# Hybrid decoder trunk step: recalibrated planner, FP32 stages in any unit, convolution as a side job

## The chip, the cores and the metric

The kernel runs on one core of one Trainium2 chip. The metric is the device time of one execution in microseconds (us), the median of several runs; less is better. Everything is computed in float32.

## The reference, cut to what matters

One layer on 256 prompt rows and 8 x 8 sample rows (T = 320 rows of 2048 columns). The parts that the change touches:

```python
def mixer_projections(x, g_mix, w_in, g_q_swa, g_k_swa, g_q_x):
    z = rmsnorm(x, g_mix) @ w_in
    b, c, hc, q, k, v, qx = jnp.split(z, IN_SPLITS, axis=-1)
    ...
    return b, c * hc, q, k, v, qx

def short_conv(u_ext, w):                  # CONV_K = 3 taps, 512 columns
    out = w[0] * u_ext[:, 0:length]
    for i in range(1, CONV_K):
        out = out + w[i] * u_ext[:, i:i + length]
    return out

y_conv = b * short_conv(u_ext, conv_w)     # u_ext: u = c * hc behind two earlier rows
y_swa = swa_prompt(...) / swa_sample(...)  # window 128, rel_bias(dist, table), sinks
y_x = cross_attention(qx, mk, mv)          # 256 memory tokens, 4 heads
x = x + concat([y_conv, y_swa, y_x]) @ w_out
x = x + jnp.square(relu(rmsnorm(x, g_mlp) @ w_up)) @ w_down
```

The new convolution rows and the keys and values of the windows are returned as well.

## The kernel before, in words

Activations lie transposed, 128 features on the partitions and the 320 rows along the free side. Each large product is made of three F32R matmuls (high x high, high x low, low x high). The weights come in pieces of 256 x 512 (512 KB). ACT copies a piece to its high part (`wh`), DVE subtracts that to give its low part (`wl`, `split_piece`, lines 415 to 447). There are four raw buffers and four split buffers; the load of a piece into a raw buffer is issued on SP's queue behind the DVE operation that frees the buffer.

The weights' columns are worked through in groups of 512: x-queries, keys and values, memory keys, memory values, queries (two groups), then C, H, B of the convolution, then w_out, w_up, w_down. A group is a list of units. A standard unit is 12 matmuls of 320 columns; a unit of the memory groups is 6 matmuls of 512 columns. `run_unit` (486) writes a unit's matmuls into the program, then splits a further piece, and then `boundary` (478) writes what has been held back: evacuations of PSUM, low parts, and one `step` of the side jobs.

All smaller work is side jobs: Python generators (heads' norms, the bias table, the memory's norm, attention of prompt and samples, outputs) that `Side.step` (218) advances once behind each unit. A `yield n` sleeps n steps. A job's small matmuls thus stand in TensorE's queue between two units, and each engine works through its queue in the order in which the program was written.

When a job may go on is decided while the program is written, by a planner's clock, the class `Pace` (93). It keeps one clock for each engine and one for the transfers; `cost` (106) gives the time of an operation, `load` (135) that of a transfer: bytes at a rate, and then `LAG` more until the tile counts as landed (2.0 for raw weights). `after(*tiles)` (272) lets a job sleep until all its tiles are written by 0.2 us or more on TensorE's planned clock. `bank(every)` (276) fetches a PSUM bank for a small product; with `every=2`, the default, only at an even step. The loops at 885 and 919 (memory attention of the samples) also wait for an even step.

Jobs that the prediction speaks of: `x_job` (563) splits x and ends at step 7. `bias_job` (1062) starts at step 8: a DVE memset of the tile `z`, POOL's loads of the table into it and of a one-hot matrix into `w`, `yield 4`, `after`, a bank, then one product of 33 rows. `cross_sample` (863) has four batches of keys and four of values, two 256 KB tiles each; the first two batches are loaded at the start, each later one when a batch has been used. `h_evac` (1153) takes a column block of h out of PSUM, multiplies it with C's block and forms the three taps of the convolution; behind its fourth block it starts `conv_out_job` (1170), which issues an output on POOL's queue. `pre_late` (1220) issues the copies of the old caches (out_old_k, out_old_v) on the same queue. `b_evac` (1182) needs the convolution's result. `zs` are ten tiles for such results.

Of the kernel before, what the change touches and what calls it, by code (L numbers as in the profile page):

```python
# [12 lines left out]
ALU = mybir.AluOpType  # L13
AX = mybir.AxisListType

P = 128
# [15 lines left out]
NEG = -1e30  # L32

NW2 = 12
LAG = 6.0
WARM = 10
C_B, C_C, C_H, C_Q, C_K, C_V, C_X = 0, 512, 1024, 1536, 2560, 2816, 3072

# [54 lines left out]
class Pace:  # L93
# [12 lines left out]
    def cost(self, eng, op, out, ins):  # L106
        n = max(a.free_size() for a in [out] + ins)
        if eng == "pe":
            n = out.free_size()
            if ins[0].dtype == F32R:  # L110
                return 0.0033 + n / 2400.0
            quarter = 0.25 if out.partition_size() == 32 else 1.0
            return 0.0009 * n if op == "transpose" else max(0.11, n / 600.0) * quarter
        if eng == "act":
            return 0.1 + n * 0.00083
        if eng == "dve":
            return 0.08 + n * 0.00104
        return 0.1 + n * 0.0025

    def issue(self, eng, op, out, ins):  # L120
# [13 lines left out]

    def load(self, out):
        start = max(self.clock["dma"], self.clock["pe"])
        self.clock["dma"] = start + out.free_size() * 4 * out.partition_size() / 330e3
        self.wrote[out.name] = (self.clock["dma"] + (2.0 if out.name.startswith("raw") else LAG), "dma")

    def ready(self, tiles):  # L140
# [6 lines left out]
class Paced:  # L147
# [3 lines left out]
    def __getattr__(self, op):  # L151
        f = getattr(self.engine, op)
        if not callable(f) or op == "preload_act_table_set":
            return f

        def issue(*args, **kw):
            aps = [a for a in list(kw.values()) + list(args) if isinstance(a, bass.AP)]
            out = kw["out"] if "out" in kw else args[0]
            if op == "dma_start":
                if out.name not in self.pace.dram:  # L160
                    self.pace.load(out)
            else:
                if "accum_out" in kw:
                    self.pace.wrote[kw["accum_out"].name] = (self.pace.clock[self.name] + 0.5, self.name)
                self.pace.issue(self.name, op, out, [a for a in aps if a is not out])
            return f(*args, **kw)  # L166

        return issue
# [79 lines left out]
def trunk_step(ctx: ExitStack, tc: tile.TileContext, I, O):  # L248
    nc = tc.nc
    pace = Pace()  # L250
    side = Side(NW2, pace)
# [16 lines left out]
    ax = Slots(axp, "ax", 4, pace.idle)  # L268
    zs = Slots(zp, "z", 10)
# [3 lines left out]
        while not pace.ready(tiles):  # L273
            yield 1

    def bank(every=2):

        while side.now % every:
            yield 1
        t = ax.get([P, 512])  # L280
        while t is None:
            yield every
            t = ax.get([P, 512])
        return t

    def zt(cols=336):
        return zs.need([P, 336])
# [43 lines left out]
    def gcol(name, i=0):  # L331
        return cols[:, col[name] + i:col[name] + i + 1]
# [6 lines left out]
    st = {}  # L339
# [233 lines left out]
    def mean_rsqrt(out, sq):  # L573

        yield from after(sq)
        bk = yield from bank(1)
        yield from mean_over(bk, sq, mean_d)
        y = yield from zt()
        yield from newton_terms(y[:, 0:T], out, bk[:, 0:T])
        ax.put(bk)  # L580
        dve.tensor_scalar(out=y[:, 0:T], in0=y[:, 0:T], scalar1=-0.5, scalar2=None, op0=ALU.mult)
        dve.scalar_tensor_tensor(out=out, in0=out, scalar=-3.0, in1=y[:, 0:T], op0=ALU.add, op1=ALU.mult)
        zs.put(y)
# [52 lines left out]
    def start_head(name, ps, gain, dest):  # L636
        early = "rb" not in side.flags
        home = w2 if early else zs
        z = home.must([P, 336])
        if early:  # L640
            side.held += 1
            act.activation(out=z[:, 0:T], in_=ps, func=AF.Copy)
        else:
            dve.tensor_tensor(out=z[:, 0:T], in0=ps, in1=rb, op=ALU.mult)

        def gen():
            if early:
                while "rb" not in side.flags:
                    yield 1
                dve.tensor_tensor(out=z[:, 0:T], in0=z[:, 0:T], in1=rb, op=ALU.mult)  # L650
            while side.now < turn[0] or turn[1] == 2:
                yield 1
            turn[0] = side.now + 2
            turn[1] += 1
            y = yield from zt()
            yield from after(z)
            act.activation(out=y[:, 0:T], in_=z[:, 0:T], func=AF.Square)
            yield 1
            yield from after(y)
            bk = yield from bank(1)  # L660
            yield from mean_over(bk, y[:, 0:T], mean_h)
            a = yield from zt()
            yield from newton_terms(y[:, 0:T], a[:, 0:T], bk[:, 0:T])
            ax.put(bk)
            dve.scalar_tensor_tensor(out=z[:, 0:T], in0=z[:, 0:T], scalar=gain, in1=y[:, 0:T],
                                     op0=ALU.mult, op1=ALU.mult)
            zs.put(y)
            dest(lambda out, v: dve.scalar_tensor_tensor(out=out, in0=v(a), scalar=-3.0, in1=v(z),
                                                         op0=ALU.add, op1=ALU.mult))
            zs.put(a)  # L670
            home.put(z)
            side.held -= int(early)
            turn[1] -= 1

        side.add(name, gen())
# [131 lines left out]
    def cross_prompt(h):  # L807
        yield from after(st["qxT"])
        split_both(lambda m: m[:, 4 + h, 0:TP], st["qxT"][:, h, :])
        yield 1  # L810
        yield from after(S1l[:, 4 + h, :], S1l[:, 0, :])
        bk = yield from bank(1)
        for t in range(2):
            three(bk[:, t * 256:(t + 1) * 256], [m[:, 4 + h, t * P:(t + 1) * P] for m in (S1h, S1l)],
                  [m[:, h, 0:MEM] for m in (S1h, S1l)], True, True)
        yield 1
        p = yield from half()
        den = sm()
        cut = [slice(t * 256, (t + 1) * 256) for t in range(2)]
        yield from cross_softmax([(p[:, c], bk[:, c]) for c in cut], den)  # L820
        ax.put(bk)
        yield from after(p)
        bk = yield from bank()
        for kb in range(2):
            for t in range(2):
                pe.transpose(bk[:, kb * 256 + t * P:kb * 256 + (t + 1) * P],
                             p[:, t * 256 + kb * P:t * 256 + (kb + 1) * P], ident)
        yield 1
        w2.put(p)
        pt = []  # L830
        for _ in range(2):
            t = yield from w2.need([P, 512], F32R)
            pt.append(t)
        act.activation(out=pt[0], in_=bk, func=AF.Copy)
        dve.tensor_tensor(out=pt[1], in0=bk, in1=pt[0].bitcast(F32), op=ALU.subtract)
        ax.put(bk)
        yield from after(pt[1])
        bk = yield from bank(1)
        for kb in range(2):
            v = [m[:, 8 + kb * 2 + h // 2, h % 2 * P:(h % 2 + 1) * P] for m in (S1h, S1l)]  # L840
            three(bk[:, 0:TP], v, [t[:, kb * 256:(kb + 1) * 256] for t in pt], kb == 0, kb == 1)
        yield 1
        w2.put(*pt)
        yield from put_mix(lambda m: m[:, 12 + h, 0:TP], bk[:, 0:TP])
        ax.put(bk)
# [17 lines left out]
    def cross_sample(f):  # L863
# [18 lines left out]
        for b in range(4):  # L882
            cur = queue.pop(0)
            yield from after(*cur)
            while side.now % 2:
                yield 1
            for h in range(XH):
                pe.matmul(out=sb[h * 32:(h + 1) * 32, 0:MEM], lhsT=qm[:, h * P + b * 32:h * P + b * 32 + 32],
                          rhs=cur[h // 2][:, (h % 2) * MEM:(h % 2 + 1) * MEM], start=b == 0, stop=b == 3,
                          tile_position=(0, h * 32), skip_group_check=True)  # L890
            w2.put(*cur)
            yield from load()
# [23 lines left out]
        for b in range(4):  # L916
            cur = queue.pop(0)
            yield from after(*cur)
            while side.now % 2:
                yield 1  # L920
            for kb in range(2):
                for h in range(XH):
                    c = h * 32
# [229 lines left out]
    def h_evac(m, ps):  # L1153
# [5 lines left out]
        dve.tensor_tensor(out=u[:, m, 2:258], in0=z[:, 0:TP], in1=u[:, m, 2:258], op=ALU.mult)  # L1159
        us = usample(m)[:, :, 2:10]  # L1160
        dve.tensor_tensor(out=us, in0=per_batch(z[:, TP:T]), in1=us, op=ALU.mult)
        dve.tensor_scalar(out=z, in0=u[:, m, 0:336], scalar1=gcol("conv_w", m), scalar2=None, op0=ALU.mult)
        for i in (1, 2):
            dve.scalar_tensor_tensor(out=z, in0=u[:, m, i:i + 336], scalar=gcol("conv_w", 4 * i + m), in1=z,
                                     op0=ALU.mult, op1=ALU.add)
        st["y"][m] = z
        if m == 3:
            side.add("convout", conv_out_job())

    def conv_out_job():  # L1170
        cu = yield from zt()
# [8 lines left out]
        yield 1  # L1180

    def b_evac(m, ps):
        side.until(["cp"])
        y = st["y"][m]
        z = zs.must([P, 336])
        dve.tensor_tensor(out=z[:, 0:T], in0=ps, in1=rb, op=ALU.mult)
# [217 lines left out]
```

## Time and profile before

| | |
|---|---|
| median of 3 runs | 1320.77 us (1320.54 to 1321.83) |
| the profiled execution, its own time | 1322.82 us |
| its span | 1320.7 us |
| TensorE (PE) busy | 1311.3 us, 8956 matmuls |
| weight loads (PEld) busy | 1289.5 us |
| VectorE (DVE) busy | 674.7 us, 1025 instructions |
| ScalarE (ACT) busy | 541.3 us, 801 instructions |
| GpSimd (POOL) busy | 18.1 us, 37 instructions |
| bytes moved | 217.03 MB, mean 164 GB/s |
| chain that ended last | PE 93%, DVE 3%, DMA 2%, ACT 1%, issue 1% |

Matmuls overlap in the array, so the duration of one (0.31 us) is longer than the distance between two starts. In the timelines a row is start, duration, engine, operation, tile written <- tiles read, count, and in brackets the engine's idle time before it and what ended it. The tiles' names: `mm` and `ax` are PSUM banks of the large and of the small products, `S0h`, `S0l`, `S1h`, `S1l` the split activations, `w` the 12 tiles of the attention, `lx` and `z` work tiles. All operations pass through one helper, so the line is 166 nearly everywhere.

### The profile page before, as it was taken

The numbers are of one execution on the slowest core, as the hardware profiler recorded it, in microseconds if no ns is written. First come the engines' busy times: TensorE is split into PE (matmuls) and PEld (weight loads), VectorE is DVE, ScalarE is ACT, GpSimd is POOL, SyncE is SP. The second block draws the span as 40 slices with busy tenths as digits, with TensorE's granted clock in tenths as the row PEclk, the third lists the DMA queues.
The fourth block names the chain that finished last, engine by engine and source line by source line (L and its number), as shares of the span: only waits on it lengthen the run. The fifth ranks groups of instructions, "written<-read, shape, count | busy, mean of one in ns | idle before, by whom it ended". The sixth has DMA issues, their size and how long they took to land.

```text
span 1320.7 us, 21556 instructions
## 1 busy us (share of the span) xinstructions
PE 1311.3 (99%) x8956; PEld 1289.5 (98%) x8956; DVE 674.7 (51%) x1025; ACT 541.3 (41%) x801; POOL 18.1 (1%) x37
## 2 busy tenths in 40 slices
PE   9999999999999999999999999999999999999999
PEld 9988999889999999999999999999999999999998
DVE  6877665766566444443344543434444344444343
ACT  7684563334355444332334433234442223443321
POOL 1011000000000000000000000000000000000000
PEclk9999999989999999999999999999999999999999
DMA  8668454456344444445444445444444444444552
GB/s 313 236 200 286 167 188 159 178 184 228 108 153 159 148 157 144 144 144 160 156 148 144 141 149 166 151 145 142 147 159 158 144 153 135 155 153 155 171 172 72
DMA packets 65489, 217.03 MB, mean 164 GB/s; under 512 B 8438, under 2 KB 10718, under 8 KB 65361
## 3 DMA queue, kind: packets, MB, share of 16 engines
q1 hardware_dynamic: 63184, 210.14, 48.1%
q0 software_dynamic: 1776, 5.26, 1.1%
q8 instruction: 70, 1.15, 0.4%
q10 hardware_dynamic: 432, 0.28, 0.1%
q14 instruction: 27, 0.21, 0.0%
HBM read 211.53 MB, written 7.65 MB: 166 GB/s over the span
## 4 chain that ended last, share of the span: by engine, by line
PE 93%; DVE 3%; DMA 2%; ACT 1%; issue 1%; SPq 0%; DVEq 0%; ACTq 0%
PE mm L166 90%; PE ax L166 3%; DMA raw<-in_w_in 2%; DVE z L166 1%; DVE wl L166 1%; ACT wh L166 1%; DVE lx L166 0%; ACT lx L166 0%; DVE S1l L166 0%; DVE w L166 0%; DVE sm L166 0%; ACT z L166 0%; ACT S0h L166 0%; DVE S0l L166 0%; ACT S1h L166 0%
## 5 line engine op out<-in xcount | busy, mean ns | idle before, releaser
L166 DVE TENSOR_TENSOR wl<-raw,wh 128x1024 fp32r<-128x1024 f32 (+1 forms) x362 | 436.1, 1217 | 487.3 <-ACT wh L166 476.4
L166 ACT ACTIVATE wh<-raw 128x1024 fp32r<-128x1024 f32 (+1 forms) x362 | 374.5, 1050 | 629.1 <-PE mm L166 581.1
L166 PE MATMUL mm<-S0h,wh 128*128 128x320 f32 x1472 | 455.8, 311 | 0.8 <-DVE z L166 0.4
L166 PE MATMUL mm<-S0h,wl 128*128 128x320 f32 x1472 | 453.6, 310 | 1.1 <-DVE wl L166 1.1
L166 PE MATMUL mm<-S0l,wh 128*128 128x320 f32 x1472 | 453.7, 310 | 0.3 <-DVE S0l L166 0.3
L166 PE MATMUL mm<-S1h,wh 128*128 128x320 f32 x1280 | 397.4, 310 | 0.0
L166 PE MATMUL mm<-S1h,wl 128*128 128x320 f32 x1280 | 395.5, 309 | 0.0
L166 PE MATMUL mm<-S1l,wh 128*128 128x320 f32 x1280 | 395.5, 309 | 0.0
L166 PEld LDWEIGHTS mm<-S0h,wh 128*128 128x128 f32 x1472 | 276.5, 188 | 3.3 <-issue 1.4
L166 PEld LDWEIGHTS mm<-S0h,wl 128*128 128x128 f32 x1472 | 276.6, 188 | 1.3 <-DVE wl L166 1.3
L166 PEld LDWEIGHTS mm<-S0l,wh 128*128 128x128 f32 x1472 | 276.7, 188 | 0.6 <-DVE S0l L166 0.6
L166 PEld LDWEIGHTS mm<-S1h,wh 128*128 128x128 f32 x1280 | 240.4, 188 | 0.2
L166 PEld LDWEIGHTS mm<-S1l,wh 128*128 128x128 f32 x1280 | 240.4, 188 | 0.2
L166 PEld LDWEIGHTS mm<-S1h,wl 128*128 128x128 f32 x1280 | 240.3, 188 | 0.0
L166 DVE TENSOR_TENSOR lx<-mm,lx 128x320 f32<-128x320 f32 (+1 forms) x97 | 46.8, 485 | 77.1 <-PE mm L166 77.0
L166 ACT ACTIVATE z<-z 128x320 f32<-128x320 f32 (+1 forms) x118 | 55.0, 470 | 64.4 <-DVE z L166 63.2
L166 DVE TENSOR_TENSOR S1l<-z,S1h 128x320 fp32r<-128x320 f32 x68 | 33.4, 491 | 51.1 <-ACT S1h L166 51.1
L166 ACT ACTIVATE S1h<-z 128x320 fp32r<-128x320 f32 x68 | 32.1, 472 | 7.5 <-DVE z L166 5.5
L166 DVE SCALAR_TENSOR_TENSOR z<-mm,r2b 128x320 f32<-128x320 f32 x64 | 31.0, 484 | 0.0
L166 PE MATMUL mm<-wh,S1h 128*128 128x512 f32 x64 | 25.6, 400 | 0.0
L166 PE MATMUL mm<-wl,S1h 128*128 128x512 f32 x64 | 25.0, 391 | 0.0
L166 PE MATMUL mm<-wh,S1l 128*128 128x512 f32 x64 | 25.0, 391 | 0.0
(162 smaller groups left out, 432.5 us busy)
## 6 DMA issues: line engine op xcount, KB each, us to landing
raw<-in_w_up SPq DMA_DIRECT2D x128, 512.0 KB, 3.3
raw<-in_w_down SPq DMA_DIRECT2D x128, 512.0 KB, 3.3
raw<-in_w_in SPq DMA_DIRECT2D x54, 512.0 KB, 4.1
raw<-in_w_out SPq DMA_DIRECT2D x32, 512.0 KB, 3.7
raw<-in_w_mem_k SPq DMA_DIRECT2D x8, 512.0 KB, 6.4
raw<-in_w_mem_v SPq DMA_DIRECT2D x8, 512.0 KB, 4.3
w<-in_cmk SPq DMA_DIRECT2D x16, 256.0 KB, 5.8
w<-in_cmv SPq DMA_DIRECT2D x16, 256.0 KB, 5.1
```

The source lines that it names most:

```text
L166: return f(*args, **kw)
```

## The change

The planner's constants are changed, `bank` asks for a free bank at every step, the waits for even steps in `cross_sample` go, and the three taps of the convolution move from `h_evac` to a side job `conv_job`, for which `b_evac` waits. `ax.need` is the loop that tries `get` at every step.

```diff
@@ -32,7 +32,7 @@
 NEG = -1e30
 
 NW2 = 12
-LAG = 6.0
+LAG = 3.5
 WARM = 10
 C_B, C_C, C_H, C_Q, C_K, C_V, C_X = 0, 512, 1024, 1536, 2560, 2816, 3072
 
@@ -108,13 +108,13 @@
         if eng == "pe":
             n = out.free_size()
             if ins[0].dtype == F32R:
-                return 0.0033 + n / 2400.0
+                return 0.0135 + n / 2400.0
             quarter = 0.25 if out.partition_size() == 32 else 1.0
             return 0.0009 * n if op == "transpose" else max(0.11, n / 600.0) * quarter
         if eng == "act":
-            return 0.1 + n * 0.00083
+            return 0.2 + n * 0.00084
         if eng == "dve":
-            return 0.08 + n * 0.00104
+            return 0.16 + n * 0.00105
         return 0.1 + n * 0.0025
 
     def issue(self, eng, op, out, ins):
@@ -134,7 +134,7 @@
 
     def load(self, out):
         start = max(self.clock["dma"], self.clock["pe"])
-        self.clock["dma"] = start + out.free_size() * 4 * out.partition_size() / 330e3
+        self.clock["dma"] = start + out.free_size() * 4 * out.partition_size() / 410e3
         self.wrote[out.name] = (self.clock["dma"] + (2.0 if out.name.startswith("raw") else LAG), "dma")
 
     def ready(self, tiles):
@@ -161,8 +161,10 @@
                     self.pace.load(out)
             else:
                 if "accum_out" in kw:
-                    self.pace.wrote[kw["accum_out"].name] = (self.pace.clock[self.name] + 0.5, self.name)
+                    self.pace.wrote[kw["accum_out"].name] = (self.pace.clock[self.name] + 0.9, self.name)
                 self.pace.issue(self.name, op, out, [a for a in aps if a is not out])
+                if "accum_out" in kw:
+                    self.pace.clock[self.name] += 0.19
             return f(*args, **kw)
 
         return issue
@@ -273,15 +275,8 @@
         while not pace.ready(tiles):
             yield 1
 
-    def bank(every=2):
-
-        while side.now % every:
-            yield 1
-        t = ax.get([P, 512])
-        while t is None:
-            yield every
-            t = ax.get([P, 512])
-        return t
+    def bank():
+        return ax.need([P, 512])
 
     def zt(cols=336):
         return zs.need([P, 336])
@@ -573,7 +568,7 @@
     def mean_rsqrt(out, sq):
 
         yield from after(sq)
-        bk = yield from bank(1)
+        bk = yield from bank()
         yield from mean_over(bk, sq, mean_d)
         y = yield from zt()
         yield from newton_terms(y[:, 0:T], out, bk[:, 0:T])
...
@@ -882,8 +877,6 @@
         for b in range(4):
             cur = queue.pop(0)
             yield from after(*cur)
-            while side.now % 2:
-                yield 1
             for h in range(XH):
                 pe.matmul(out=sb[h * 32:(h + 1) * 32, 0:MEM], lhsT=qm[:, h * P + b * 32:h * P + b * 32 + 32],
                           rhs=cur[h // 2][:, (h % 2) * MEM:(h % 2 + 1) * MEM], start=b == 0, stop=b == 3,
@@ -916,8 +909,6 @@
         for b in range(4):
             cur = queue.pop(0)
             yield from after(*cur)
-            while side.now % 2:
-                yield 1
             for kb in range(2):
                 for h in range(XH):
                     c = h * 32
@@ -1159,13 +1150,21 @@
         dve.tensor_tensor(out=u[:, m, 2:258], in0=z[:, 0:TP], in1=u[:, m, 2:258], op=ALU.mult)
         us = usample(m)[:, :, 2:10]
         dve.tensor_tensor(out=us, in0=per_batch(z[:, TP:T]), in1=us, op=ALU.mult)
-        dve.tensor_scalar(out=z, in0=u[:, m, 0:336], scalar1=gcol("conv_w", m), scalar2=None, op0=ALU.mult)
-        for i in (1, 2):
-            dve.scalar_tensor_tensor(out=z, in0=u[:, m, i:i + 336], scalar=gcol("conv_w", 4 * i + m), in1=z,
-                                     op0=ALU.mult, op1=ALU.add)
-        st["y"][m] = z
+        zs.put(z)
         if m == 3:
-            side.add("convout", conv_out_job())
+            side.add("convy", conv_job())
+
+    def conv_job():
+        u = st["u"]
+        for m in range(4):
+            z = yield from zt()
+            dve.tensor_scalar(out=z, in0=u[:, m, 0:336], scalar1=gcol("conv_w", m), scalar2=None, op0=ALU.mult)
+            for i in (1, 2):
+                dve.scalar_tensor_tensor(out=z, in0=u[:, m, i:i + 336], scalar=gcol("conv_w", 4 * i + m), in1=z,
+                                         op0=ALU.mult, op1=ALU.add)
+            st["y"][m] = z
+            yield 2
+        side.add("convout", conv_out_job())
 
     def conv_out_job():
         cu = yield from zt()
@@ -1180,7 +1179,7 @@
         yield 1
 
     def b_evac(m, ps):
-        side.until(["cp"])
+        side.until(["cp", "convy"])
         y = st["y"][m]
         z = zs.must([P, 336])
         dve.tensor_tensor(out=z[:, 0:T], in0=ps, in1=rb, op=ALU.mult)
```

The hunks left out replace `bank(1)` by `bank()`.

## Rows read from the trace of the kernel before

**Rows 1.** Busy time by stretch: us, busy (instructions) per engine, granted clock, DMA.

```profile
80.00:240.00 160.00, 159.97 (x1160) 148.11 (x1159) 100.53 (x203) 85.08 (x164) 10.08 (x20) 1.00 0.64 216
240.00:290.00 50.00, 46.55 (x332) 42.65 (x331) 33.33 (x95) 15.15 (x37) 1.71 (x3) 0.93 0.46 156
...
420.00:1317.50 897.50, 897.43 (x6119) 897.16 (x6118) 390.99 (x449) 320.56 (x384) 0.00 (x0) 1.00 0.46 150
```

**Rows 2.** TensorE in order of time, the three waits between 255 and 275 us.

```profile
256.68 0.41 PE L166 MATMUL mm<-S0h,wh 128*128 128x320 f32 x1 [0.45 <-DVE z L166]
...
260.05 0.42 PE L166 MATMUL mm<-S0h,wl 128*128 128x320 f32 x1 [1.06 <-DVE wl L166]
...
274.98 0.58 PE L166 MATMUL ax<-vns,z 64*128 64x128 f32 x1 [1.95 <-DVE z L166]
```

**Rows 3.** Busy time of the stretch behind the last of these waits.

```profile
274.70:281.50 6.80, 6.52 (x35) 5.30 (x36) 1.96 (x6) 0.55 (x2) 0.00 (x0) 0.50 0.55 174
```

**Rows 4.** DVE in order of time, one evacuation of h.

```profile
252.40 0.48 DVE L166 TENSOR_TENSOR z<-mm,rb 128x320 f32<-128x320 f32 x1
252.92 0.56 DVE L166 TENSOR_TENSOR lx<-z,lx 128x256 f32<-128x256 f32 x2
253.51 0.40 DVE L166 TENSOR_SCALAR z<-lx,cols 128x336 f32<-128x336 f32 x1
253.94 1.17 DVE L166 SCALAR_TENSOR_TENSOR z<-lx,cols,z 128x336 f32<-128x336 f32 x2
```

**Rows 5.** The chain that ended last: start, us, engine and what.

```profile
258.78 1.22 DVE wl L166
...
261.75 9.58 DMA raw<-in_w_in
```

**Rows 6.** POOL in order of time, 170 to 290 us.

```profile
260.89 0.54 POOL L166 DMA_DIRECT2D out_conv<-z  x1 [84.14 <-DVE z L166]
```

**Rows 7.** DMA issues of the whole span: count, KB each, median us to landing.

```profile
w<-in_cmk SPq DMA_DIRECT2D x16, 256.0 KB, 5.8
...
out_old_k<-in_cache_swa_k POOLq DMA_DIRECT2D x1, 960.0 KB, 8.9
...
z<-in_rel_bias_table POOLq DMA_DIRECT2D x1, 1.0 KB, 5.3
```

**Rows 8.** DMA issues near 92.2 us.

```profile
w<-in_cmk SPq DMA_DIRECT2D x2, 256.0 KB, 4.8
```

**Rows 9.** POOL in order of time, the bias table's load.

```profile
26.99 0.55 POOL L166 DMA_DIRECT2D z<-in_rel_bias_table  x1 [24.98 <-DVE z L166]
```

**Rows 10.** TensorE in order of time, the bias product and the norm of x.

```profile
34.73 0.81 PE L166 MATMUL ax<-w,z 33*8 33x384 f32 x2
35.47 0.41 PE L166 MATMUL mm<-S0h,wh 128*128 128x320 f32 x1
...
40.48 0.42 PE L166 MATMUL ax<-z,mean_d 128*128 128x320 f32 x1 [0.64 <-DVE z L166]
```

**Rows 11.** TensorE in order of time, where the samples' loads are entered.

```profile
88.55 0.39 PE L166 MATMUL mm<-wh,S1h 128*128 128x512 f32 x1
...
89.92 0.45 PE L166 MATMUL ax<-z,mean_h 128*128 128x320 f32 x2
...
149.58 0.31 PE L166 MATMUL mm<-S0h,wh 128*128 128x320 f32 x1
...
202.00 0.28 PE L166 MATMUL ax<-S1h,S1l 128*128 128x256 f32 x1
```

**Rows 12.** SP's queue in order of time, the same loads.

```profile
91.73 1.91 SPq L166 DMA_DIRECT2D w<-in_cmk  x4
...
99.32 4.18 SPq L166 DMA_DIRECT2D raw<-in_w_in  x3
...
151.15 1.81 SPq L166 DMA_DIRECT2D w<-in_cmk  x4
...
203.41 2.25 SPq L166 DMA_DIRECT2D w<-in_cmv  x4
```

More of the change, by code (lines that the diff above doesn't have):

```diff
@@ L659, in gen @@
             yield from after(y)
-            bk = yield from bank(1)
+            bk = yield from bank()
             yield from mean_over(bk, y[:, 0:T], mean_h)
@@ L811, in cross_prompt @@
         yield from after(S1l[:, 4 + h, :], S1l[:, 0, :])
-        bk = yield from bank(1)
+        bk = yield from bank()
         for t in range(2):
@@ L837, in cross_prompt @@
         yield from after(pt[1])
-        bk = yield from bank(1)
+        bk = yield from bank()
         for kb in range(2):
```

## The prediction

> **What bounds the kernel now.** I read busy time by stretch first, then TensorE's own waits, then the chain of work that ended last. The last 897.5 us hold 6119 matmuls back to back, 897.5 / 6119 = 146.7 ns each at the full clock [rows 1]. Nothing in the change touches that stretch, so what it does lies in the first 420 us. There TensorE is almost full too (159.97 of the 160 us from 80 to 240 us), apart from one hole: between 240 and 290 us it is busy for 46.55 of 50 us at a mean granted clock of 0.93 [rows 1]. The hole has three waits, 0.45 us for the evacuation of a PSUM bank, 1.06 us for a weight's low part, and 1.95 us for a softmax result [rows 2], and behind the last wait a stretch of 6.8 us at 0.50 of the clock, the lower of its two levels [rows 3]. Half of the 6.52 us busy there is lost, 3.3 us. The hole costs 0.45 + 1.06 + 1.95 + 3.3 = 6.7 us, and it is most of what any reordering here can win.
>
> **What the change removes.** The hole begins on DVE. Each evacuation of h takes 0.48 + 0.56 + 0.40 + 1.17 = 2.6 us there [rows 4]; four come in four units of 12 x 146.7 ns = 1.76 us, so 10.4 us of DVE work meet 7.0 us of TensorE. The low parts of the next weight pieces stand behind them in DVE's queue; their raw buffers come free late, and the piece asked for at 261.75 needs 9.58 us [rows 5] because POOL issues out_conv at 260.89 [rows 6] and at once behind it the two copies of the old caches, 960 KB each; one takes 8.9 us [rows 7]. As a side job the 0.40 + 1.17 us leave the evacuation: 1.05 us per unit of 1.76, and the 6.3 us come back one column block every second unit beside the first eight units of B, where a piece of weights (1.22 us of DVE [rows 5]) per 3.5 us leaves room. I let 6.2 of the 6.7 us go (bounds 2.5, if DVE stays behind because the sample softmaxes crowd there too, and 6.7). What is late next: conv_out now ends nine units or more later, so the copies fall near 270 to 278 us; they stretch a load by up to 9.58 us again, but four raw and four split pieces, 4 x 3.5 us, hide it as long as DVE is not behind. B's evacuation waits for the side job, twelve units after it starts, and the job needs about eight: nothing. If zs runs out of tiles there, up to four steps of about 2 us each would show.
>
> **What the new clock moves.** The planner only decides behind which unit a small product is put; TensorE then takes its queue in order, and if the operand has not come, everything behind it waits. Costs for DVE and ACT go up by about 0.09 us per operation and a unit of TensorE grows from 1.64 to 1.76 us on the planner's clock; for chains of ACT and DVE the two cancel, and I cost them at 0 (bounds -0.5 and +1.5, two of the waits that the first 80 us show now, 0.64 us for the longest [rows 10]). For products that wait for a transfer they do not cancel: LAG falls by 2.5 us, 4 tiles get 0.6 us cheaper, the longer unit gives the rest. By the planner's rules, worked out by hand:
>
> The bias product. The bias job issues its table loads at step 8 and yields 4. Until now the queue of transfers in the planner's clock (9.8 MB at 330 GB/s, plus 6.0) held the product to step 15, the even rule to 16. Now 26.2 + 3.5 + 0.2 = 29.9 stands against 31.5 on TensorE's planned clock at step 12, so it goes behind unit 12 instead of 16. In the trace it runs at 34.73 [rows 10]; four units earlier is 34.73 - 48 x 0.1467 = 27.7. But POOL, which waits for DVE's memset of that tile, issues the table's load only at 26.99 [rows 9], and it needs 5.3 us [rows 7]; the one-hot matrix goes 0.55 us behind it, so the operands are there at 32.4. TensorE stands for 4.7 us. Of that, the later waits for rb's chain (0.64 us in the row at 40.48 [rows 10], about 1.1 us with the smaller ones near it) are absorbed. Cost 3.6 us. The clock: the one fall in this trace came in a gap of about 2 us and cost 3.3 us; I take 2 (0 to 3.3), as part of the slow time lies in the wait itself.
>
> The memory attention of the samples. Its products wait for four 256 KB tiles at a time. First pair: the loads are entered at the boundary before the unit that runs from 88.55 to 89.92, six matmuls of 0.228 us [rows 11]. The planner now wants 0.3 + 1.3 + 3.7 = 5.3 us, which is four such units with two small means of 2 x 0.147 us between: TensorE is there at 94.6. The second tile is issued at about 92.2 [rows 12] and takes 4.8 [rows 8]: 97.0. Wait 2.4 us (bounds 0 and 3.4, with the median of 5.8 [rows 7]). Second pair: its loads stand on SP behind the weight piece of 99.32 [rows 12], so the second tile starts near 100.3 and lands at 105.1 to 106.1; TensorE is there at about 104.0: 1.5 us (0 to 2.1). Other half, first pair: entered at 149.58 [rows 11]; three units and four means later is 155.5; the second tile, issued at 151.6 [rows 12], lands at 156.4 to 157.4: 1.5 us (0 to 2.5). Its values: entered at 202.1 [rows 11], three units and one pair of means later is 207.7; issued at 204.0 [rows 12] plus 4.8 to 5.8 gives 208.8 to 209.8: 1.6 us if the planner takes three units, 0 if four, so 1.0. Together 6.4 us (1 to 10). These four may drop the clock as well, at 3.3 us each: I take 1.5 for all (0 to 6.6).
>
> The Trainium skill's "DMA: Bandwidth & Descriptors" ("Anatomy of one DMA") puts a transfer at about 2 us and its bytes at 436 GB/s; an estimate from it is 2.6 us for 256 KB, by which LAG 3.5 is ample, the 6.4 us fall away and the sum is 1322.5. The rows give 4.8 to 5.8 us after the issue, and the issue itself 2 to 3.6 us after the planner's point, so here the trace speaks against it.
>
> FP32 stages in any unit. The first F32R matmul behind an FP32 product takes 0.41 us in place of 0.31 [rows 10], 0.1 us for each entry; about eight more entries, as pairs of batches split: 0.8 us (0 to 1.5).
>
> **Sum.** 3.6 + 2 + 6.4 + 1.5 + 0.8 - 6.2 = +8.1 us. The profiled execution took 1322.82 us (span 1320.7 and 2.1 around it), so 1330.9; it is 2.05 us above the median of 1320.77, and against that median the sum is 1328.9. I predict 1329 (its own range 1324 to 1338).
>
> **Rivals.** First, faster: the hole closes and the loads come in time. For it: SP issues a load as soon as its buffer is free, so a TensorE that has once waited gives all later loads a lead; and if DVE clears the bias job's memset sooner, the table is early. Then the hole gives -6.7, the bias product at most +2, the tiles +1: 1320.8 - 3.7 = 1317. It decides at whether the tables land before about 29.5 us; POOL's row at 26.99, which waits for DVE [rows 9], speaks against it. 0.15.
>
> Second, no change: the bias product costs 3.6 with the clock kept, the tiles 2 because one wait covers the next, the entries 0.8, the hole gives 6.2: 1321. It needs a clock that does not fall in a wait of 4.7 us where it fell in one of 2. 0.15.
>
> Third, slower still: DVE stays behind (B's units carry weights, convolution and four softmaxes at once), so only 2.5 us of the hole go, and the tiles' waits drop the clock twice: 3.6 + 3.3 + 8 + 6.6 + 0.8 - 2.5 = +19.8, 1341. 0.10. The Trainium skill's "TensorE: Matmul & The Clock Gate" ("HAM oscillation — how this bites in real kernels") says that a matmul stream that stops for transfers falls back to the lower clock and begins its next work there. By that rule each of the four tile waits pays and the sum comes near this case; the trace agrees for the wait at 272 to 275 us, and not for the shorter ones before it.
>
> That the change does not do what it says is part of the first case: were the product of the table to stay behind unit 16, its 5.6 us would go and the sum be 1323.3.
>
> **How the numbers follow.** My forecast has 0.60, the rivals 0.15, 0.15 and 0.10. Runs of this kernel tell 0.2%, 2.6 us, from no change. The forecast and the third rival are slower: 0.70; same 0.15; faster 0.15. The range runs from the first rival to the third: 1317 to 1342.
>
> **What would show it.** The 33-row product behind 144 matmuls instead of 192, with an idle of 4 to 5 us ended by a transfer of the bias table; waits of TensorE on cmk or cmv where there are none now; no wait on DVE and a clock of 1.00 between 240 and 290 us; out_conv on POOL past 265 us; the last stretch at 146.7 ns as before. I am wrong if the bias product has no wait, if the four tile waits sum to under 2 us, or if the hole is still there.

## The result and the profile after

The changed kernel takes 1330.99 us (median of four, 1330.05 to 1331.92), the kernel before 1321.30 beside it; the ratio is 1.0069 [1.0051, 1.0087]: slower by 0.7%, with an interval clear of 1. The profiled execution took 1331.12 us, its span is 1329.0 us, 8.3 more than before. Of 52 executions of the kernel before that were timed beside the experiments, ten ran at a mean clock of 1.000 and took 1318.8 to 1319.8 us, so the 3.3 us of the clock in its hole are not paid every time.

Busy time by stretch of the kernel after; the columns are those of [rows 1], and 80 to 240, 240 to 290 and the dense end answer to its rows.

```profile
27.60:33.20 5.60, 0.38 (x4) 0.14 (x3) 3.42 (x4) 5.25 (x7) 3.70 (x7) 0.76 0.94 311
30.50:37.40 6.90, 4.25 (x13) 3.00 (x14) 5.50 (x10) 4.00 (x6) 1.01 (x3) 0.51 0.67 223
80.00:240.00 160.00, 155.81 (x1086) 138.53 (x1085) 99.80 (x216) 83.11 (x166) 10.18 (x20) 0.99 0.61 202
139.80:143.20 3.40, 3.13 (x37) 2.65 (x38) 2.75 (x6) 0.00 (x0) 0.00 (x0) 0.50 0.76 220
240.00:290.00 50.00, 50.00 (x369) 48.43 (x368) 35.58 (x90) 19.98 (x48) 0.00 (x0) 1.00 0.44 148
...
420.00:1325.00 905.00, 905.00 (x6173) 905.00 (x6172) 397.68 (x461) 325.58 (x394) 0.00 (x0) 1.00 0.46 149
```

The end runs at 905.00 / 6173 = 146.6 ns per matmul, as before. The hole of 240 to 290 us is gone: 50.00 us busy for 46.55, at a clock of 1.00 for 0.93. What was won there is lost ahead of it. TensorE stands nearly all of the 5.6 us from 27.6 to 33.2, is at half its clock from 30.5 to 37.4, and loses 4.2 us between 80 and 240 us, where it had lost nothing.

TensorE's waits over the whole span of the kernel after: line and tile, what ended the wait, us in total, times, longest.

```profile
PE ax L168 <- DMA w<-in_c_hot: 5.2, 1, 5.2
PE ax L168 <- DVE w L168: 2.3, 1, 2.3
PE ax L168 <- DMA w<-in_cmk: 1.1, 1, 1.1
...
PE ax L168 <- DMA w<-in_csk: 0.6, 1, 0.6
...
```

TensorE in order of time in the kernel after: the bias product, both pairs of memory keys, the products with the memory values, which waited for DVE, and a later batch of keys.

```profile
27.62 0.31 PE L168 MATMUL mm<-S0h,wl 128*128 128x320 f32 x1
33.16 1.44 PE L168 MATMUL ax<-w,z 33*8 33x384 f32 x2 [5.22 <-DMA w<-in_c_hot]
...
103.39 2.41 PE L168 MATMUL ax<-w,w 128*32 128x256 f32 x16
...
111.99 2.56 PE L168 MATMUL ax<-w,w 128*32 128x256 f32 x16
...
140.07 1.93 PE L168 MATMUL ax<-w,w 128*32 128x128 f32 x32 [2.33 <-DVE w L168]
...
170.78 1.28 PE L168 MATMUL ax<-w,w 128*32 128x256 f32 x8 [1.07 <-DMA w<-in_cmk]
```

The bias product answers to the row at 34.73 of [rows 10]: it now stands behind the unit that ends at 27.6, and 5.5 us pass before it starts. The sixteen products of a pair of key batches took 1.07 us in the kernel before (its row for the first pair, the first line of the next fence) and take 2.41 and 2.56 now: in the first pair they start as four groups of four, one for each 256 KB tile, at 103.39, 103.81, 104.48 and 105.17, as the tiles land one by one (issued from 98.57 on, 4.8 us median). The list of waits puts nothing down for these two. Such a hidden wait is seen only where the busy time of a group is held against the same group elsewhere.

First the kernel before, TensorE's first pair, then SP's queue of the kernel after, the loads of those pairs; the last two rows answer to [rows 12].

```profile
98.81 1.07 PE L166 MATMUL ax<-w,w 128*32 128x256 f32 x16
```

```profile
92.11 6.40 SPq L168 DMA_DIRECT2D raw<-in_w_mem_v  x3
98.57 1.85 SPq L168 DMA_DIRECT2D w<-in_cmk  x4
104.34 1.86 SPq L168 DMA_DIRECT2D raw<-in_w_in  x2
106.30 1.81 SPq L168 DMA_DIRECT2D w<-in_cmk  x4
```

DVE and POOL of the kernel after: the copies of the convolution's cached rows, one of the taps as a side job (with [rows 4]), POOL's bias loads [rows 9] and its output of the convolution with the old caches behind it [rows 6].

```profile
135.95 0.41 DVE L168 COPY lx<-w 128x16 f32<-128x16 f32 x4 [5.42 <-DMA w<-in_cconv]
...
273.88 0.39 DVE L168 TENSOR_SCALAR z<-lx,cols 128x336 f32<-128x336 f32 x1
274.30 1.17 DVE L168 SCALAR_TENSOR_TENSOR z<-lx,cols,z 128x336 f32<-128x336 f32 x2
```

```profile
27.81 0.55 POOL L168 DMA_DIRECT2D z<-in_rel_bias_table  x1 [25.79 <-DVE z L168]
28.35 0.54 POOL L168 DMA_DIRECT2D w<-in_c_hot  x1
...
290.52 0.54 POOL L168 DMA_DIRECT2D out_conv<-z  x1 [110.02 <-DVE z L168]
```

The row at 135.95 is the wait that the prediction does not have: DVE stood 5.42 us for a 32 KB load, the low parts and evacuations behind it came late, and TensorE's row at 140.07 paid with 2.33 us and a stretch at half the clock, in which 3.13 us were busy and so about 1.6 lost.

### The profile page after: what moved, and what is told of

It reads as the page before. It is cut to its first block, busy times and chain, and to the rows that moved or that the text cites. A ratio compares the mean times of both kernels' runs of the same rounds, so it can differ in the third digit from the quotient of the medians.

```text
span 1329.0 us, 21560 instructions
## 1 busy us (share of the span) xinstructions
PE 1315.0 (99%) x8956; PEld 1291.0 (97%) x8956; DVE 674.9 (51%) x1025; ACT 541.2 (41%) x801; POOL 18.2 (1%) x37
## 4 chain that ended last, share of the span: by engine, by line
PE 88%; DMA 1%; issue 0%; DVE 0%; SPq 0%; ACT 0%; DVEq 0%
PE mm L168 85%; PE ax L168 3%; DMA w<-in_cmk 0%; DMA w<-in_csk 0%; SPq L168 0%; DVE wl L168 0%; DVE z L168 0%; ACT z L168 0%; DVE lx L168 0%; DVEq L1399 0%; DVE w L168 0%; DVE S1l L168 0%; ACT wh L168 0%
```

## The experiments

The first theory: the loss is early products that wait for transfers, the hole's closing is worth about what was predicted, and the parts add. The rival to the last point: a wait gives later loads a lead, so the parts do not add. Each kernel was timed in five rounds or more beside the kernel before (1321.1 to 1322.0 us).

**e1, the convolution alone.** The kernel before with only the side job.

```diff
     def h_evac(m, ps):
...
-        dve.tensor_scalar(out=z, ..., op0=ALU.mult)
-        for i in (1, 2):
-            dve.scalar_tensor_tensor(out=z, ...)
-        st["y"][m] = z
+        zs.put(z)
...
+    def conv_job():        # for m in range(4): the taps of block m, then yield 2
...
-        side.until(["cp"])
+        side.until(["cp", "convy"])
```

> The kernel before with the convolution's side job alone (conv_job, b_evac waits for it), planner and even steps as before. Theory: the hole at 255 to 282 us (three waits and 6.8 us at half clock) goes, worth 5 to 6.7 us: 1314.5 to 1316.5 against 1321. Rival (DVE stays behind, as softmaxes and weights fill the same units): the hole stays or moves, 1319 to 1323.

Measured: 1316.18 us, ratio 0.9960 [0.9948, 0.9973]; span 1314.7, 6.0 under the span before, clock 1.000. Held. It beats both kernels; of the others here only e8, 0.6 us behind, is as fast. In its stretch of the old hole, columns as in [rows 1]:

```profile
240.00:290.00 50.00, 50.00 (x375) 46.70 (x374) 39.13 (x111) 18.50 (x42) 1.71 (x3) 1.00 0.50 168
```

**e2, the bias product back behind unit 16.** The kernel after with

```diff
         pool.dma_start(out=gkx, in_=I["g_k_x"].to_broadcast([P, P]))
-        yield 4
+        yield 8
```

> The changed kernel with the bias job sleeping 8 steps in place of 4, so that its product stands behind unit 16 again; all else as changed. Theory: the 5.2 us wait and the 2.1 us lost to the lower clock go, 1.2 us of later waits come back: 6 us, from 1331 to 1325. Rival (the ACT and DVE chain of the first 100 us sets the time there, and a late start of TensorE is absorbed): 1329 or more.

Measured: 1330.34 us, ratio 1.0070 [1.0058, 1.0083]; span 1330.3. Wrong by 5 us; the rival's number came true. The profiled execution is the longest of the five. TensorE, SP's queue and DVE at the same place, in this kernel:

```profile
34.61 0.81 PE L168 MATMUL ax<-w,z 33*8 33x384 f32 x2
...
102.39 0.74 PE L168 MATMUL ax<-w,w 128*32 128x256 f32 x4 [3.63 <-DMA w<-in_cmk]
103.94 2.81 PE L168 MATMUL ax<-w,w 128*32 128x256 f32 x12 [0.81 <-DMA w<-in_cmk]
```

```profile
93.03 0.42 SPq L168 DMA_DIRECT2D w<-in_c_own  x1
...
98.43 0.34 SPq L168 DMA_DIRECT2D raw<-in_w_in  x1
98.81 1.86 SPq L168 DMA_DIRECT2D w<-in_cmk  x4
```

```profile
97.18 1.23 DVE L168 TENSOR_TENSOR wl<-raw,wh 128x1024 fp32r<-128x1024 f32 x1 [3.04 <-ACT wh L168]
```

The bias product has no wait now, and a wait of 4.4 us turns up 70 us later. TensorE is at the product by 98.8 (102.39 - 3.63), in the kernel after at about 103.4, but the keys go out no earlier, at 98.81 for 98.57. That is not because the weights' loads kept their old times: they moved with TensorE. The 34th of them on SP goes out at 92.64 here and at 98.19 in the kernel after, 5.55 us earlier. It is the plan that moved. The bias job ends later, and the load of c_own, whose job waits for it, stands behind the 34th weight load in place of the 31st. The planner put the keys' loads behind the 35th in place of the 34th, and their product behind 522 large matmuls in place of 510. The 35th goes out about 6 us behind the 34th in both kernels (98.43 here, 104.34 there). Here it went out when DVE's low part of 97.18 had ended (98.41); that had waited 3.04 us for ACT's high part, which ACT began at 96.10 behind 4.7 us of work on the memory keys. In the kernel after the keys are ahead of that late load, in e2 they are behind it. So e2 is not the kernel after with one wait less; this is read from the rows and not tested with the plan held still.

**e3, e2 with the old LAG.**

```diff
-LAG = 3.5
+LAG = 6.0
```

> As the one with the late bias product, and LAG back at 6.0; the rate of 410 GB/s, the new costs, FP32 in any unit and the convolution's job stay. Theory: the waits on cmk, csk and on DVE held by the load of cconv go as well (1.3 + 1.6 + 2.3 and 1.7 of clock + 1.1 + 0.6 = 8.6 us): 1316, 1314 to 1318, as the convolution's job alone. Rival (FP32 in any unit or the new costs cost time themselves): 1321 or more.

Measured: 1319.60 us, ratio 0.9986 [0.9977, 0.9995]; span 1317.5, clock 1.000. That is 10.7 under e2: with the bias product out of the way, LAG is nearly all of the rest of the loss on transfers (0.6 us of waits on the keys are left). It stays 3.4 above e1, and more than expected; its waits are on ACT for attention weights (1.6 us in two) and its last attention products run until 363 us, where e1's run until 346.

**e4, the even steps back.** The kernel after with `bank(every=2)` and the two loops of before.

```diff
-    def bank():
-        return ax.need([P, 512])
+    def bank(every=2):
+        while side.now % every:
+            yield 1
...
             yield from after(*cur)
+            while side.now % 2:
+                yield 1
```

> The changed kernel with the even steps back (bank(every=2) and the two loops of cross_sample); LAG 3.5 and all else as changed. Theory: the bias product stays at step 12, so its loss stays; products that wait for loads go up to one unit later, so part of these waits goes: 1327 to 1331. Rival (FP32 entries in any unit are the loss): 1321 to 1323.

Measured: 1336.41 us, ratio 1.0120 [1.0101, 1.0140]; span 1339.2. Wrong: it costs 5.4 more. From its list of waits, of an execution of 1341.66 us, the longest of the five:

```profile
PE ax L168 <- DMA w<-in_c_hot: 6.4, 1, 6.4
PE ax L168 <- DVE w L168: 4.4, 1, 4.4
PE ax L168 <- DMA w<-in_cmv: 2.8, 2, 2.7
...
```

The even rule does not make up for the new constants. It delays the attention too, whose products then meet a DVE that is behind (4.45 us in the row at 370 us).

**e5, the bias product alone.** e1 with the product four units earlier, every other planner's constant as before.

```diff
         yield 4
-        yield from after(bt, hot)
-        bk = yield from bank()
+        bk = yield from bank(1)
         pe.matmul(out=bk[0:NH, 0:384], lhsT=bt[0:33, 0:8], ...)
+        yield 4
```

> The kernel with the convolution's job alone (1316.2 us), and in it only the bias product moved from behind unit 16 to behind unit 12, where it meets its operands too early; what follows on that product stays where it was. Theory: the wait of about 5 us and about 2 us of lower clock come, 1.5 us of later waits (norm of x) go: 1321 to 1323, as nothing behind it waits for loads that could use the lead. Rival (the ACT and DVE chain of the first 100 us absorbs a late TensorE): 1316 to 1318.

Measured: 1322.39 us, ratio 1.0007 [0.9998, 1.0015]; span 1320.3, 5.6 over e1 (6.2 in the medians). Held. The product in order of time, and the stretch behind it (columns as in [rows 1]):

```profile
32.75 1.44 PE L166 MATMUL ax<-w,z 33*8 33x384 f32 x2 [5.14 <-DMA w<-in_c_hot]
```

```profile
32.00:39.00 7.00, 6.25 (x20) 5.00 (x21) 3.20 (x5) 0.96 (x3) 0.00 (x0) 0.51 0.57 195
```

Here the keys' loads and their product stand where they stand in e1, behind the 33rd weight load and behind 516 large matmuls. The first keys' load and the product, in e1 and then in e5:

```profile
92.30 1.97 SPq L166 DMA_DIRECT2D w<-in_cmk  x4
99.40 1.07 PE L166 MATMUL ax<-w,w 128*32 128x256 f32 x16
```

```profile
97.93 1.84 SPq L166 DMA_DIRECT2D w<-in_cmk  x4
104.99 1.07 PE L166 MATMUL ax<-w,w 128*32 128x256 f32 x16
```

The load goes out 5.63 us later and the product starts 5.59 later: from one to the other it is 7.10 us in e1 and 7.06 in e5. TensorE's wait of 5.14 us gave this load no lead; SP's queue moved with TensorE (the 34th weight load from 94.38 to 99.88). So the wait costs 5.6 us alone, and e2, which gains 0.7 in the medians, does not show what it costs in the kernel after, as its plan is another.

**e6, LAG and the rate alone.** e1 with

```diff
-LAG = 6.0
+LAG = 3.5
...
- ... / 330e3
+ ... / 410e3
```

> The kernel with the convolution's job alone (1316.2 us), and in the planner only LAG 3.5 and 410 GB/s; old costs, even steps. Theory (the transfers' figures are the loss): products meet loads too early, the bias product among them: 1322 to 1328. Rival (the loss comes from the other constants or the free steps): 1315 to 1318.

Measured: 1327.53 us, ratio 1.0055 [1.0042, 1.0068]; span 1324.7, 10.0 over e1 (11.4 in the medians). Held. From its list of waits:

```profile
PE ax L166 <- DMA w<-in_c_hot: 4.9, 1, 4.9
PE ax L166 <- DMA w<-in_cmk: 1.2, 2, 0.6
...
PE ax L166 <- DVE w L166: 0.9, 1, 0.9
...
```

**e7, the costs of the engines alone.** e1 with the new costs of TensorE, ACT, DVE and of sums, and one more change that this needs: the evacuation of the memory keys also waits for the memory's norm.

```diff
-                return 0.0033 + n / 2400.0
+                return 0.0135 + n / 2400.0
...
-            return 0.08 + n * 0.00104
+            return 0.16 + n * 0.00105
...
+        side.until(["mem"])
```

> The kernel with the convolution's job alone (1316.2 us), and in the planner only the new costs of PE, ACT, DVE and of accumulating operations; LAG 6.0, 330 GB/s, even steps. The memory keys' evacuation also waits in the program for the memory's norm, which the new layout finishes later. Theory: the higher costs and the longer unit cancel: 1314 to 1318. Rival (chains get more steps, the last attention products come too late for w_out): 1319 to 1325, with waits behind 340 us.

Measured: 1324.56 us, ratio 1.0026 [1.0015, 1.0038]; 8.4 over e1 in the medians; the profiled execution, 1322.48 us, is the shortest of the eleven, and its span of 1320.4 is 5.7 over e1's. The rival held. TensorE in order of time, and DVE ahead of it:

```profile
351.94 0.63 PE L168 MATMUL ax<-ident,w 128*128 128x128 f32 x4 [2.47 <-DVE w L168]
353.38 1.59 PE L168 MATMUL ax<-w,vnat 128*128 128x256 f32 x4 [0.82 <-ACT w L168]
```

```profile
349.06 1.22 DVE L168 TENSOR_TENSOR wl<-raw,wh 128x1024 fp32r<-128x1024 f32 x1
...
350.58 0.62 DVE L168 TENSOR_SCALAR w<-w,sm 128x256 f32<-128x256 f32 x2
```

With dearer operations the softmax chains are given more units, the attention ends at 366 us instead of 346, and its last pieces come without the distance that hides a chain: a softmax stands behind a low part on DVE, TensorE waits 2.47 us, and the clock is at half for 3.4 us after it. What the added wait for the memory's norm does to this was not run apart.

**e8, any unit alone.** e1 with `bank()` free at every step and without the two even loops.

```diff
-    def bank(every=2):
...
+    def bank():
+        return ax.need([P, 512])
...
-            while side.now % 2:
-                yield 1
```

> The kernel with the convolution's job alone (1316.2 us), and only FP32 stages in any unit (bank() at every step, no even steps in cross_sample). Theory: entries into FP32 cost 0 to 1 us, some products come a unit earlier and one or two may wait for a load: 1315 to 1319. Rival (free steps are a gain by themselves, as the even-step variant of the changed kernel was 5 us slower): 1311 to 1314.

Measured: 1316.77 us, ratio 0.9970 [0.9958, 0.9982]; span 1314.7, the same as e1's. Held: 74 groups of small products for 62, at no cost that the span shows.

**e9, e2 with the old LAG for the keys' and values' tiles only.**

```diff
+                    pace.wrote[t.name] = (pace.wrote[t.name][0] + 2.5, "dma")
```

> The changed kernel with the bias product behind unit 16 (1330.3 us, in which TensorE waits 6.4 us on cmk and runs at half clock for 6.8 and 3.4 us behind it), and LAG 6.0 for the cmk and cmv tiles alone. Theory (the waits on these tiles are what the early wait for the table had hidden): they go, with their clock, about 9 us: 1320 to 1323. Rival (each wait taken away comes back at the next product that depends on a transfer): 1326 or more.

Measured: 1323.38 us, ratio 1.0017 [1.0008, 1.0026]; span 1320.2. It is 7.0 under e2, of the 10.7 that LAG as a whole gives in e3; it is 0.4 above the range expected, and the rival did not hold. These tiles are most of what LAG costs in this plan. Most of the waiting left is for DVE (1.02 us at 355.42 and 1.62 at 366.06), near the end of an attention that runs until 362 us, late as in e3 and e7; on transfers a smaller wait is left:

```profile
105.30 1.29 PE L168 MATMUL ax<-w,w 128*32 128x256 f32 x8 [0.88 <-DMA w<-in_cmk]
```

**e10, the convolution's rows later.** The kernel after with eight more units between the load and DVE's copies.

```diff
         sp.dma_start(out=cc[:, 0:64], ...)
+        yield 8
         yield from after(cc)
```

> The changed kernel, in which the job that loads cconv sleeps 8 steps before its DVE copies, so that DVE does not stand 5.4 us in front of them. Theory: the 2.3 us wait of TensorE on DVE at 140 us and the 3.4 us of half clock behind it go: 4 us, from 1331 to 1327. Rival (the wait had given the later cmk loads their lead, and they wait longer now): 1329 to 1331.

Measured: 1326.62 us, ratio 1.0046 [1.0034, 1.0059]; span 1324.6. The theory held: the copies run without a wait and TensorE's 2.33 us are gone; the later wait on keys fell too, from 1.1 to 0.5. DVE's row:

```profile
142.92 0.40 DVE L168 COPY lx<-w 128x16 f32<-128x16 f32 x4
```

## Why the prediction came out right, step by step

The time, 1329 for 1331, and the side it was on were right. Of the five terms of the sum the hole and the bias product held, the entries were small as said, and two were off in opposite ways, the tiles by 4.0 us too much and the chains by 3.9 too little. That the two cancel is luck, and without it the sum would have been some 4 us off.

- **The hole: -6.2.** Held: e1's span fell by 6.0, and no wait on DVE is left between 240 and 290 us. The output of the convolution moved from 260.89 to 290.52, further than the 270 to 278 forecast, and took the copies of the caches with it, without a wait there.
- **The bias product: +3.6 and +2 for the clock.** Held: a wait of 5.2 us for 4.7, POOL's load at 27.81 for 26.99, and 6.90 us at 0.51 of the clock with 4.25 busy, so about 2.1 lost. Alone it costs 5.6 (e5).
- **The memory tiles: +6.4 and 1.5 for the clock.** The mechanism held for three places of four, at a smaller size: 2.41 - 1.07 = 1.3 for the first pair (2.4 predicted), 2.56 - 1.07 = 1.5 for the second (1.5), 1.1 for the other half (1.5), none for its values (1.0), and no fall of the clock at these: 3.9 for 7.9. The first pair's times were both off, by nearly as much. Its loads went out from 98.57 on, for 91.73 before: the bias wait had moved the weights' loads too (the 33rd at 95.45 for 90.08), and one more of them stands ahead on SP (34 for 33). TensorE was at the product at 103.39, for 94.6 predicted: the bias wait had moved it, and the product stands behind 510 large matmuls, two units later than the prediction had it.
- **The chains of ACT and DVE: 0.** This is the step that failed. It looked only at products that wait for an operand and not at an engine that waits for a transfer in the middle of its queue. DVE's copies of the cached rows are entered by LAG as well; they waited 5.42 us, and all behind them with them. It cost 2.33 us and about 1.6 for the clock; e10 shows 4.4 by taking it away, with the 0.6 less on the keys. In other plans the wait is there too: DVE stands 4.68 us for this load in e2 (and TensorE 2.1 behind it), 2.6 in e6, 0.7 in e3 with the old LAG, and not at all in the kernel before. The engines' costs, also put at 0 with bounds of -0.5 and +1.5, cost 5.7 of span and more by themselves (e7), through attention that ends 20 us later; in the kernel after TensorE has no wait between 290 and 420 us, so this loss is not in its time.
- **The entries: +0.8.** At most: 0.0 in span, 0.6 in time (e8).

Against e1 the kernel after is 14.3 longer in span: 5.6 as the bias product costs alone leave 8.7, which is what the prediction put on tiles, clock and entries (6.4 + 1.5 + 0.8), but the trace fills it with 3.9 on the keys, 0.6 on the samples' keys (the row of in_csk), and 3.9 behind the convolution's rows: 8.4 together. The sums meet, and their parts do not.

The prediction's first rival says that a TensorE that has once waited gives all later loads a lead. The runs do not bear it out: in e5 the keys' load moved with the wait (7.06 us ahead of its product, 7.10 in e1), and in the kernel after the 34th weight load goes out 5.55 us later than in e2, where TensorE does not wait for the table. What did make the parts depend on each other is the planner: a constant or a job that changes can move the loads and products behind it, as in e2. So the parts need not add: e6's 10.0 and e7's 5.7 make 15.7 for a bundle of 14.3, and e7's loss is not in the bundle's trace.

The page that the prediction weighed against the rows, the Trainium skill's "DMA: Bandwidth & Descriptors" ("Anatomy of one DMA"), by which LAG 3.5 would be ample, does not hold here: with the smaller LAG, and the new rate, e6 is 10.0 us longer than e1 in span, and with the old LAG e3 is 10.7 us faster than e2. The 256 KB tiles took 5.5 us from issue to landing (median of 16 in the kernel after), and the issue itself stood behind weight pieces. That section of the Trainium skill gives its figures for transfers issued from GpSimd, and these go out on SP's queue; but POOL's own load of 1 KB took 5.1 us.

```profile
w<-in_cmk SPq DMA_DIRECT2D x16, 256.0 KB, 5.5
...
w<-in_cconv SPq DMA_DIRECT2D x1, 32.0 KB, 5.4
z<-in_rel_bias_table POOLq DMA_DIRECT2D x1, 1.0 KB, 5.1
```

The Trainium skill's "TensorE: Matmul & The Clock Gate" ("HAM oscillation — how this bites in real kernels") says that a stream which stops for transfers begins its next work at the lower clock. The trace agrees for the wait of 5.22 us, and for the one of 2.33, which was for DVE (0.51 and 0.50 at their ends and behind them); the wait of 1.07 us at 170.78 had no such end: from 170.7 to 176 the clock is 1.00.

What stays open: why the even steps cost 5.4 us in e4 and nothing in e8 was read from e4's waits alone and not tested; what the bias wait costs in the kernel after, with its plan held still, was not run; and e3's last 3.4 us were not taken apart beyond the later attention.

## What to carry to other kernels

A planner's constant for a transfer must cover the time from where the load is written in the program to where it has landed, with the queue ahead of it, not the time of one transfer: 2.5 us taken off it, with a faster rate, cost 10.0 us of span here (e6). An edit that moves one job can move all that is planned behind it, so price a wait in a kernel in which nearly all else stays where it was: e5 holds the plan and shows 5.6 us, e2 does not and shows nothing. When a change has several parts, run each alone: the one part that moved work off a crowded engine was worth 6 us, and the bundle hid it.

## What was not expected of the hardware

The list of waits leaves out waits inside a group of small products: 1.3 and 1.5 us showed only as a longer busy time of sixteen products (2.41 and 2.56 us for 1.07). And between the weight pieces the one load of 32 KB took as long from issue to landing (5.4 us) as the 256 KB tiles do (5.5 us, median).
